# A list schedule for five engines: a price for every change of tile shape on TensorE, and a table that shifts streams of work in the order

## The chip, the cores and the metric

The kernel runs on one core of a Trainium2 chip. Time is in device microseconds (us) of one execution, lower is better. The engines are named as the profile names them: PE is TensorE (matmul), PEld its weight loads, DVE is VectorE, ACT is ScalarE, POOL is GpSimd, and SP issues the DMAs. Each engine works through its own row of instructions in order and waits on semaphores for the others.

## The reference

Two layers of a transformer block over 1024 tokens of width 1024, in float32. Each layer takes a normed and modulated copy of x, projects it, runs three mixers on it, and adds their result and that of a gated feed-forward to x:

```python
for l in range(DEPTH):
    mod = jax.nn.silu(c) @ ada_w[l] + ada_b[l]
    sh1, sc1, g1, sh2, sc2, g2 = jnp.split(mod[:, None, :], 6, axis=-1)
    h = rms_norm(x, norm1_g[l]) * (1.0 + sc1) + sh1
    z = h @ w_in[l]
    ...
    o_a = dsa_mixer(...)
    o_b = rwkv7_mixer(...)
    o_c = nsa_mixer(...)
    mixed = jnp.concatenate([o_a, o_b, o_c], axis=-1) @ w_out[l]
    x = x + g1 * mixed
    h = rms_norm(x, norm2_g[l]) * (1.0 + sc2) + sh2
    gate, up = jnp.split(h @ ffn_wi[l], 2, axis=-1)
    x = x + g2 * ((jax.nn.silu(gate) * up) @ ffn_wo[l])
```

dsa_mixer is an attention over the 256 best keys of each query by an index score. rwkv7_mixer is a linear recurrence with a 64 x 64 state for each of 8 heads. nsa_mixer adds up an attention over compressed blocks, one over the 16 best blocks and one over a window of 512.

## The kernel before

**Tiling and stages.** The tokens are worked in two halves of 512, with the width on the partitions: x is eight tiles of 128 x 512. A dense product (`dense`) adds up in one accumulator `mm` of 128 x 512, of which there are two. Each operand is split into a high and a low part in fp32r (`whi`, `wlo` from a loaded tile `wraw`; `hh`, `hl` from the normed x; `acthi`, `actlo` and `ohi`, `olo` likewise), and each product is three matmuls: high by high, low by high, high by low. The stages of the main stream are `("D", l, h)`, the projection of half h in layer l, and `("F", l, h)`, output projection and feed-forward, in the order D00, D01, F00, D10, F01, D11, F10, F11.

**The other streams.** The attention blocks (tiles `at`, `p`, `pt`, `pT`, `po`), the units of the recurrence (`am`, `X`, `TX`, `av`, `WU`, `MN`, `S`, `Y`), the top-k searches (`score`, `junk`, `sel`, `tk_...`), and the modulation of the second layer (`macc`, sums of loaded tiles `ada` on DVE) run as streams of their own beside the main one. A norm (`norm`) is a stream too: PE sums the squares `nsq` into `ss`, DVE takes the inverse root in twelve short steps on `ss` and `nex`, PE broadcasts it as `rb`, and DVE and ACT make `nt`, `hh` and `hl` of it. The small steps on PE use a part of the array: S, X, TX are 64 x 64, `po` and Y 128 x 64, `ss` 128 x 32. In the scan S, each of eight steps needs `sh`, which DVE makes of the step before. `z` is made in two halves: ACT writes one (`z<-mm,omu`), DVE adds the other (`z<-mm,vec,z`) and by that frees the accumulator.

**What sets the order.** The kernel runs its streams twice through generators. The first run plans buffers; in the second, `Program` records every instruction with its dependencies in the order in which the streams were taken up (`Rec`, numbered `r.n`). `Program.order` then makes the final order: a list schedule that steps through the five engines, and on each takes, of the records whose operands are ready, the one with the lowest number. `Chip` holds its prices. On PE, `Chip.is_part` tells a record on the full array from one on a part of it; if the next record is of the other kind, one of the present kind that stands at most LATER = 100 numbers behind is taken first. A change from full to part is charged 0.095 us and one back 0.045, the first full record after a part is charged 0.105 more, and a change between two part shapes nothing. `Program.issue` (line 697) writes all instructions out, so every row of the trace has that line and is told by its tiles.

Of the kernel before, what the change touches and what calls it, by code (L numbers as in the profile page):

```python
# [497 lines left out]
class Rec:  # L498
    __slots__ = ("key", "name", "a", "k", "cost", "deps", "n", "users", "pe", "func", "port", "prio")

# [20 lines left out]
class Program:  # L521
# [32 lines left out]
    def add(self, key, name, a, k, aps, outs, cost, pe=None, port=False):  # L554
        r = Rec()
        r.key, r.name, r.a, r.k, r.cost, r.pe, r.port = key, name, a, k, cost, pe, port
        r.n, r.deps, r.users = len(self.recs), set(), []
        r.prio = self.weave.cur.prio
        r.func = a[2] if key == "S" and name == "activation" else None
# [45 lines left out]
    def order(self):  # L605

        recs, chip, LATER = self.recs, Chip(), 100

        kinds, begun = ([], []), set()
        missing = [len(r.deps) for r in recs]
        for r in recs:
            for d in r.deps:
                recs[d].users.append(r.n)
        ready = {e: [] for e in ENGINES}
        coming = {e: [] for e in ENGINES}
        at = [0.0] * len(recs)
        for r in recs:
            if not missing[r.n]:  # L620
                heapq.heappush(coming[r.key], (0.0, r.n))
        out = []
        while len(out) < len(recs):
            best = None
            for e in ENGINES:
                t = chip.free[e]
                if not ready[e]:
                    if not coming[e]:
                        continue
                    t = max(t, coming[e][0][0])  # L630
                while coming[e] and coming[e][0][0] <= t:
                    n = heapq.heappop(coming[e])[1]
                    heapq.heappush(ready[e], n)
                    if e == "PE":
                        heapq.heappush(kinds[Chip.is_part(recs[n])], n)
# [7 lines left out]
                s = max(chip.start(recs[n]), at[n])  # L643
                if s > t + 0.1 and recs[n].port:

                    for m in heapq.nsmallest(8, ready[e])[1:]:
                        if not recs[m].port and t + recs[m].cost < s + 0.1:
                            n, s = m, max(t, at[m])
                            break
                if best is None or s < best[0]:  # L650
                    best = (s, e, n)
            s, e, n = best
            if ready[e][0] == n:
                heapq.heappop(ready[e])
            else:
                ready[e].remove(n)
                heapq.heapify(ready[e])
            if e == "PE":
                begun.add(n)
            end = chip.put(recs[n], s)  # L660
            out.append((s, n))
            for u in recs[n].users:
                v = recs[u]
                at[u] = max(at[u], chip.after(recs[n], v, s, end))
                missing[u] -= 1
                if not missing[u]:
                    heapq.heappush(coming[v.key], (at[u], u))
# [30 lines left out]


ENGINES = ("PE", "V", "S", "G", "D")  # L700


class Chip:
# [5 lines left out]
    def __init__(self):  # L709
        self.free = {e: 0.0 for e in ENGINES}  # L710
        self.cells = [[0.0] * 4 for _ in range(4)]
        self.part, self.first = False, False
# [4 lines left out]
    def is_part(r):  # L717
        rows, cols, _ = r.pe
        return rows[1] - rows[0] + cols[1] - cols[0] < 8

    def start(self, r):

        t = self.free[r.key]
        if r.key == "PE":
            rows, cols, _ = r.pe
            part = self.is_part(r)
# [7 lines left out]
    def put(self, r, s):  # L734

        if r.key == "PE":
            rows, cols, c = r.pe
            while s >= (self.stretch + 1) * self.STRETCH:
# [3 lines left out]
                self.stretch += 1  # L742
            part = self.is_part(r)
# [5 lines left out]
            self.first = part  # L749
            share = 1.0 if not part else (rows[1] - rows[0]) * (cols[1] - cols[0]) / 16.0  # L750
# [7 lines left out]
            self.part = part  # L758
            self.free["PE"] = s + step + more
# [1765 lines left out]
```

## Time and profile before

| | us |
|---|---|
| median of 3 runs | 3439.8 |
| lowest and highest run | 3438.86, 3444.59 |
| profiled execution, its own time | 3442.7 |
| span of the profiled execution | 3441.0 |

The profile has the busy time of each engine, a timeline of instructions with the idle time before each and what ended it, and tables of stretches. A start on PE comes before the end of the matmul ahead, since matmuls are pipelined; the time from start to start is what a matmul takes of PE. PEclk is the granted clock as a share of 2.4 GHz; its two levels are 1.2 and 2.4 GHz. Matmuls in plain float32 stand in the trace as two records each, transposes and fp32r ones as one.

### The profile page before, as it was taken

To read this page: it belongs to the slowest core of one execution; us is meant where nothing else is said; L and a number is where in the kernel's file an instruction comes from. 1 tells how busy PE (TensorE), PEld (TensorE's weight loads), DVE (VectorE), ACT (ScalarE), POOL (GpSimd) and SP (SyncE) were. 2 spreads that over 40 slices of the span, in tenths; PEclk is the share of its full clock that TensorE was granted. 3 is DMA by queue.
4 is the path that set the end of the run, shared out by engine and by line. 5 is a ranking of instruction groups with operands and counts; after the bars stand their busy time and mean duration, and the time that the engine had idled before them with its cause. 6 is when DMAs were issued, how large, how long until landed. Compare 5 with 4: busy or idle time off the path is not lost. (4 is left out here: it accounts for less than half of the span.)

```text
span 3441.0 us, 58566 instructions
## 1 busy us (share of the span) xinstructions
PE 3215.3 (93%) x20564; PEld 2496.7 (73%) x20564; DVE 2176.2 (63%) x5705; ACT 1775.1 (52%) x3706; POOL 1488.3 (43%) x1235
## 2 busy tenths in 40 slices
PE   6898999989999998889899999899799999999999
PEld 3656776767767776767678887677577787778887
DVE  4688988898899634698952114698888853241112
ACT  3445566756674643545464234567777454343232
POOL 2433453434335444442434554443343344445554
PEclk8999999989999998999899999899999999999999
DMA  8684345445523243554223333463232222423333
GB/s 280 197 260 124 108 138 160 145 138 161 194 77 108 70 131 113 154 157 118 74 67 115 98 97 114 145 189 122 67 86 67 84 80 80 144 91 96 98 95 98
DMA packets 354755, 424.99 MB, mean 124 GB/s; under 512 B 129686, under 2 KB 167190, under 8 KB 354460
## 3 DMA queue, kind: packets, MB, share of 16 engines
q1 hardware_dynamic: 354460, 421.25, 39.9%
q8 instruction: 162, 2.65, 0.3%
q14 instruction: 133, 1.09, 0.1%
HBM read 347.06 MB, written 60.44 MB: 118 GB/s over the span
## 5 line engine op out<-in xcount | busy, mean ns | idle before, releaser
L697 POOL TENSOR_TENSOR wlo<-wraw,whi 128x512 fp32r<-128x512 f32 (+1 forms) x808 | 1072.1, 1329 | 1346.1 <-ACT whi L697 1243.1
L697 ACT ACTIVATE whi<-wraw 128x512 fp32r<-128x512 f32 (+1 forms) x808 | 500.7, 622 | 993.9 <-PE mm L697 664.6
L697 PE MATMUL mm<-hh,whi 128*128 128x512 f32 x2144 | 865.9, 405 | 38.5 <-ACT hh L697 10.4
L697 PE MATMUL mm<-hh,wlo 128*128 128x512 f32 x2128 | 847.9, 399 | 5.5 <-POOL wlo L697 5.4
L697 PE MATMUL mm<-hl,whi 128*128 128x512 f32 x2112 | 843.7, 400 | 5.5 <-DVE hl L697 3.2
L697 PEld LDWEIGHTS mm<-hh,whi 128*128 128x128 f32 x2144 | 410.5, 192 | 141.2 <-issue 16.1
L697 PEld LDWEIGHTS mm<-hh,wlo 128*128 128x128 f32 x2128 | 407.1, 191 | 101.0 <-POOL wlo L697 10.1
L697 PEld LDWEIGHTS mm<-hl,whi 128*128 128x128 f32 x2112 | 404.3, 191 | 94.6 <-issue 8.2
L697 DVE TENSOR_TENSOR sg<-sg,mm 128x512 f32<-128x512 f32 x87 | 59.5, 684 | 474.0 <-PE mm L697 473.8
L697 DVE SCALAR_TENSOR_TENSOR x<-mm,mod,x 128x512 f32<-128x512 f32 x232 | 172.9, 747 | 245.5 <-PE mm L697 244.5
L697 PE MATMUL mm<-acthi,whi 128*128 128x512 f32 x704 | 280.4, 402 | 13.9 <-DVE x L697 5.8
L697 PE MATMUL mm<-actlo,whi 128*128 128x512 f32 x704 | 277.6, 397 | 1.9 <-POOL actlo L697 1.8
L697 PE MATMUL mm<-acthi,wlo 128*128 128x512 f32 x704 | 276.6, 396 | 0.0
L697 ACT ACTIVATE p<-p,nb,rst 128x512 f32<-128x512 f32 (+3 forms) x256 | 170.6, 667 | 62.0 <-DVE nb L697 60.7
L697 ACT ACTIVATE junka<-score,tk_nt 128x512 int8<-128x512 f32 x240 | 165.9, 691 | 21.5 <-DVE tk_nt L697 16.0
L697 PEld LDWEIGHTS mm<-acthi,whi 128*128 128x128 f32 x704 | 133.3, 190 | 49.8 <-DVE x L697 6.8
L697 ACT COPY pT<-pt 128x512 f32<-128x512 f32 (+2 forms) x220 | 121.8, 588 | 70.3 <-PE pt L697 50.4
L697 PEld LDWEIGHTS mm<-actlo,whi 128*128 128x128 f32 x704 | 133.4, 190 | 31.2 <-POOL actlo L697 6.7
L697 PEld LDWEIGHTS mm<-acthi,wlo 128*128 128x128 f32 x704 | 133.5, 190 | 27.4 <-issue 0.2
L697 DVE TENSOR_SCALAR p<-p,rs 128x512 f32<-128x512 f32 (+3 forms) x288 | 151.9, 579 | 1.5 <-issue 0.9
L697 PE MATMUL pt<-c_ident,p 128*128 128x128 f32 x816 | 134.9, 282 | 14.3 <-DVE p L697 6.7
L697 PEld LDWEIGHTS pt<-c_ident,p 128*128 128x128 f32 x816 | 100.9, 143 | 48.8 <-issue 11.8
(386 smaller groups left out, 5916.7 us busy)
## 6 DMA issues: line engine op xcount, KB each, us to landing
wraw<-in_wi_dram SPq DMA_DIRECT2D x352, 256.0 KB, 2.6
ada<-in_ada_dram SPq DMA_DIRECT2D x192, 256.0 KB, 4.4
wraw<-in_win_dram SPq DMA_DIRECT2D x184, 256.0 KB, 3.2
wraw<-in_wo_dram SPq DMA_DIRECT2D x160, 256.0 KB, 2.6
x<-x SPq DMA_DIRECT2D x64, 256.0 KB, 3.7
w<-in_w_dram SPq DMA_DIRECT2D x64, 256.0 KB, 3.8
wraw<-in_wout_dram SPq DMA_DIRECT2D x64, 256.0 KB, 2.8
o_in<-o SPq DMA_DIRECT2D x32, 256.0 KB, 3.5
```

Of the source, the lines that this page charges most:

```text
L697: getattr(engines[r.key], r.name)(*[real(x) for x in r.a], **{n: real(x) for n, x in r.k.items()})
```

## The change

Nothing that is computed changes, and no tile, buffer or dependency; only the order that `Program.order` makes. Two parts of it change.

First, `Chip` tells shapes apart by rows and columns (`shape_of`) and not only full from part. Any change of shape is charged 0.095 us at its start, a full record after a change 0.105 more and a part record after a change 0.05, and a record of the present shape that stands at most 100 places behind is taken ahead of one of another shape.

Second, a record's place in line is no longer its number. Each record knows the scope of its stream (`r.scope`), and a table SHIFTS with some 110 entries adds an amount to the number of every record of a scope; the records are ranked anew by that (`rank`, `pos`). A scope ("F", 0, 0), "child", 2 is the second stream that the stage F00 started.

```diff
@@ Program.order
+        size, seen, place = {}, {}, []
+        for r in recs:
+            size[r.scope] = size.get(r.scope, 0) + 1
+        for r in recs:
+            k = seen[r.scope] = seen.get(r.scope, -1) + 1
+            by = SHIFTS.get(r.scope, (0,))
+            place.append((r.n + by[k * len(by) // size[r.scope]], r.n))
+        rank = [n for _, n in sorted(place)]
...
-                n = ready[e][0]
-                if e == "PE" and Chip.is_part(recs[n]) != chip.part:
-                    same = kinds[chip.part]
+                q = ready[e][0]
+                if e == "PE" and Chip.shape_of(recs[rank[q]]) != chip.shape:
+                    same = kinds.get(chip.shape)
                     while same and same[0] in begun:
                         heapq.heappop(same)
-                    if same and same[0] - n <= LATER:
-                        n = same[0]
+                    if same and same[0] - q <= LATER:
+                        q = same[0]
...
+SHIFTS = {
+    (('F', 0, 0), 'child', 2): (-298,), (('F', 0, 1), 'child', 1): (-20,), (('F', 0, 1), 'child', 2): (-55,),
...
+    (('F', 1, 1), 'child', 2): (-652,), ('F', 0, 0): (-99,), ('F', 0, 1): (2,), ('F', 1, 0): (6,),
...
@@ Chip
-        return rows[1] - rows[0] + cols[1] - cols[0] < 8
+        return rows[1] - rows[0], cols[1] - cols[0]
...
-            return t + (0.0 if part == self.part else 0.095 if part else 0.045)
+            return t + (0.0 if self.shape_of(r) == self.shape else 0.095)
...
-            more = 0.105 if not part and self.first else 0.0
...
-            step = c if not part or r.a[1].dtype != F32 else c / 2 + (0.0 if self.first else 0.05)
+            shape = self.shape_of(r)
+            part, changed = shape != (4, 4), shape != self.shape
+            more = 0.105 if changed and not part else 0.0
...
+            step = c if not part or r.a[1].dtype != F32 else c / 2
+            if part and changed:
+                step += 0.05
```

Three places show what becomes of the order. Numbers at the end of names tell instances apart; they differ between the two programs. The first is PE in the recurrence unit at 907 us, where S is the scan, po an attention's output and mm a dense product. Before:

```order
L697 MATMUL S_10811<-S_4718,MT_10656 64x64 x2
L697 MATMUL po_9928<-pT_10747,tm_127 64x256 x2
L697 MATMUL po_9928<-pT_10754,tm_4121 64x256
L697 MATMUL S_10811<-sh_10817,MT_10656 64x64 x2
L697 MATMUL po_9928<-pT_10754,tm_4121 64x256
L697 MATMUL po_9928<-pT_10776,tm_4121 64x256 x2
L697 MATMUL S_10811<-sh_10817,MT_10656 64x64 x2
L697 MATMUL po_9928<-pT_10826,tm_4089 64x256 x2
```

And after:

```order
L711 MATMUL S_10962<-S_4719,MT_10806 64x64 x2
L711 MATMUL po_9974<-pT_10917,tm_4092 64x256 x2
L711 MATMUL S_10962<-sh_10970,MT_10806 64x64 x2
L711 MATMUL mm_10945<-hh_9242,wlo_10802 128x512
L711 MATMUL mm_10945<-hh_9254,whi_10782 128x512
L711 MATMUL mm_10945<-hl_9260,whi_10782 128x512
L711 MATMUL mm_10945<-hh_9254,wlo_10802 128x512
L711 MATMUL mm_10945<-hh_9262,whi_10782 128x512
L711 MATMUL mm_10945<-hl_9275,whi_10782 128x512
L711 MATMUL S_10962<-sh_10970,MT_10806 64x64 x2
```

The po rows went elsewhere, and six dense rows stand between the second and the third S step where po rows of another shape stood. Over the whole order of PE, changes between a full and a part shape and back rise from 326 to 357 pairs, and changes between two part shapes fall from 266 to 164.

The second place is DVE at the norm of F00, around 765 us, where ss and nex are the chain of the norm and macc the modulation of the second layer. Before:

```order
L697 SCALAR_TENSOR_TENSOR macc_9152<-ada_9232,silu_c,macc_9152 128x512
L697 TENSOR_SCALAR m_2115_9255<-m_2115_9255 128x1
L697 SCALAR_TENSOR_TENSOR macc_9152<-ada_9118,silu_c,macc_9152 128x512
L697 TENSOR_SCALAR nb_9274<-m_2115_9255,rst_1832 128x1
L697 SCALAR_TENSOR_TENSOR macc_9152<-ada_9157,silu_c,macc_9152 128x512
L697 SCALAR_TENSOR_TENSOR nex_9204<-ss_9174,nex_9204 128x128
L697 SCALAR_TENSOR_TENSOR macc_9152<-ada_9264,silu_c,macc_9152 128x512
L697 SCALAR_TENSOR_TENSOR ss_9174<-ss_9174,nex_9204 128x128
L697 TENSOR_SCALAR macc_9284<-ada_9186,silu_c 128x512
L697 TENSOR_TENSOR ss_9174<-ss_9174,nex_9204 128x128
L697 TENSOR_TENSOR A_9289<-am_9242,c_msi 128x512
L697 SCALAR_TENSOR_TENSOR nex_9204<-ss_9174,nex_9204 128x128
```

And after:

```order
L711 TENSOR_TENSOR ss_9128<-ss_9128,nex_9149 128x128
L711 TENSOR_SCALAR junk_5859,tk_cn_1500_5860<-sel_6655,tk_tr_1507_85 128x128
L711 SCALAR_TENSOR_TENSOR nex_9149<-ss_9128,nex_9149 128x128
L711 SCALAR_TENSOR_TENSOR f_9053<-r_8955,vec,k_2076_9170 128x512
L711 ISA p_9186,m_2085_9106<-at_9174,c_mask 128x256
L711 ISA m_2085_9106 128x1
L711 SCALAR_TENSOR_TENSOR ss_9128<-ss_9128,nex_9149 128x128
L711 TENSOR_SCALAR m_2085_9106<-m_2085_9106 128x1
L711 TENSOR_TENSOR ss_9128<-ss_9128,nex_9149 128x128
L711 TENSOR_SCALAR nb_9197<-m_2085_9106,rst_1901 128x1
L711 SCALAR_TENSOR_TENSOR nex_9149<-ss_9128,nex_9149 128x128
```

Both pieces end with the chain's last step. The macc rows between the steps are gone; from the chain's first row to its last there are 40 rows before and 34 after.

The third is DVE at 2272 us, in front of the step that frees the accumulator mm (the row with `z<-mm`), with rows of the top-k ahead of it. Before:

```order
L697 TENSOR_SCALAR score_24234<-score_24234,tk_sg_5535_24682 128x512
L697 TENSOR_SCALAR score_24369<-score_24369,tk_sg_5535_24682 128x384
L697 TENSOR_SCALAR junk_24043,tk_cn_5534_24044<-sel_24760,tk_tr_5541_89 128x512
L697 SCALAR_TENSOR_TENSOR ssk_24673<-ssk_24673,kex_24771 128x128
L697 TENSOR_SCALAR score_24425<-score_24425,tk_sg_5535_24682 128x512
L697 TENSOR_TENSOR ssk_24673<-ssk_24673,kex_24771 128x128
L697 SCALAR_TENSOR_TENSOR z_24714<-mm_24599,vec,z_24714 128x511
```

And after:

```order
L711 TENSOR_SCALAR score_24216<-score_24216,tk_sg_5535_24611 128x512
L711 TENSOR_SCALAR score_24317<-score_24317,tk_sg_5535_24611 128x384
L711 TENSOR_SCALAR score_24385<-score_24385,tk_sg_5535_24611 128x512
L711 TENSOR_SCALAR score_24478<-score_24478,tk_sg_5535_24611 128x512
L711 TENSOR_TENSOR q_24630<-rt_24670,rot_24646 128x512
L711 TENSOR_SCALAR kex_24776<-ssk_24699 128x128
L711 SCALAR_TENSOR_TENSOR z_24726<-mm_24615,vec,z_24726 128x511
```

Here one more score row stands ahead of z than before.

## Rows read from the trace of the kernel before

**Rows 1.** The page, part 1: busy us of each engine, share of span, instructions

```profile
span 3441.0 us, 58566 instructions
...
PE 3215.3 (93%) x20564; PEld 2496.7 (73%) x20564; DVE 2176.2 (63%) x5705; ACT 1775.1 (52%) x3706; POOL 1488.3 (43%) x1235
```

**Rows 2.** Stretches (us; PE, PEld, DVE, ACT, POOL busy; PEclk, DMA share, GB/s), closing feed-forward

```profile
2889.00:3441.00 552.00, 531.72 (x2356) 433.01 (x2354) 131.73 (x184) 178.58 (x298) 264.31 (x211) 0.98 0.32 103
```

**Rows 3.** Stretches, the three parts in which rows move, and their sum

```profile
118.00:1263.00 1145.00, 1071.41 (x7867) 805.58 (x7866) 947.12 (x2652) 675.71 (x1505) 474.70 (x396) 0.96 0.47 144
...
1428.00:1894.00 466.00, 437.31 (x3380) 343.54 (x3379) 340.23 (x995) 232.03 (x495) 201.05 (x172) 0.97 0.38 110
...
2190.00:2889.00 699.00, 661.12 (x4574) 514.19 (x4574) 543.09 (x1527) 461.83 (x1015) 282.24 (x231) 0.97 0.34 103
...
sum 2310.00, PE 2169.84 PEld 1663.31 DVE 1830.44 ACT 1369.57 POOL 957.99; mean PE 723.28 PEld 554.44 DVE 610.15 ACT 456.52 POOL 319.33
```

**Rows 4.** Stretches, around three norms and around the longest wait

```profile
337.00:363.00 26.00, 17.47 (x164) 14.80 (x162) 26.00 (x70) 9.13 (x21) 12.68 (x13) 0.74 0.21 69
...
740.00:782.00 42.00, 26.38 (x106) 18.91 (x105) 40.54 (x95) 14.22 (x29) 16.55 (x14) 0.59 0.40 125
...
2263.00:2275.00 12.00, 4.56 (x18) 3.05 (x17) 10.50 (x30) 5.12 (x10) 6.36 (x5) 0.79 0.62 202
...
2440.00:2476.00 36.00, 21.31 (x133) 15.08 (x134) 33.04 (x101) 24.95 (x54) 8.24 (x7) 0.76 0.27 75
```

**Rows 5.** Timeline of PE (start, us, op, shapes, xcount, idle before), scan of S

```profile
907.02 0.33 PE L697 MATMUL S<-S,MT 64*64 64x64 f32 x4
...
907.29 1.08 PE L697 MATMUL po<-pT,tm 128*64 128x256 f32 x6
...
917.64 0.39 PE L697 MATMUL mm<-hl,whi 128*128 128x512 f32 x1
...
917.87 0.39 PE L697 MATMUL mm<-hh,wlo 128*128 128x512 f32 x1
...
918.19 0.33 PE L697 MATMUL S<-sh,MT 64*64 64x64 f32 x4
...
918.45 0.50 PE L697 MATMUL mm<-hh,whi 128*128 128x512 f32 x1
...
918.78 0.39 PE L697 MATMUL mm<-hl,whi 128*128 128x512 f32 x1
...
922.42 0.48 PE L697 MATMUL S<-sh,MT 64*64 64x64 f32 x4 [3.00 <-DVE sh L697]
```

**Rows 6.** Timeline of PE, a run of one part shape

```profile
335.11 1.15 PE L697 MATMUL TX<-X,Tt 64*64 64x64 f32 x32 [0.22 <-ACT X L697]
...
336.19 0.45 PE L697 MATMUL at<-K,Qhi 128*128 128x384 f32 x1
```

**Rows 7.** Groups of ACT: count, busy us, mean ns, idle before

```profile
L697 ACT ACT_TABLE_LOAD x61 | 78.3, 1283 | 6.3 <-DVE nb L697 4.6 <-PEq L2515 0.7
```

**Rows 8.** Timeline of PE, norm of the first feed-forward

```profile
751.37 0.65 PE L697 MATMUL ss<-nsq,c_ident 128*32 128x128 f32 x8
...
770.13 2.07 PE L697 MATMUL rb<-nex,c_sel 128*128 128x128 f32 x8
```

**Rows 9.** Timeline of DVE, same stretch, one of eight such rows

```profile
761.36 0.74 DVE L697 SCALAR_TENSOR_TENSOR macc<-ada,silu_c,macc 128x512 f32<-128x512 f32 x1
```

**Rows 10.** Waits of PE (us in total, times, longest us), 118:1263, then whole span

```profile
PE mm L697 <- DVE x L697: 3.2, 2, 3.0
...
PE mod L697 <- DMA ada<-in_ada_dram: 4.5, 3, 3.3
...
PE mm L697 <- DVE z L697: 10.5, 6, 6.4
```

**Rows 11.** Timelines of ACT and of PE around the longest wait

```profile
2263.09 0.63 ACT L697 ACTIVATE whi<-wraw 128x512 fp32r<-128x512 f32 x1 [5.91 <-DMA wraw<-in_win_dram]
...
2273.48 0.80 PE L697 MATMUL mm<-hh,whi 128*128 128x512 f32 x1 [6.43 <-DVE z L697]
```

More of the change, by code (lines that the diff above doesn't have):

```diff
@@ L498 @@
 class Rec:
-    __slots__ = ("key", "name", "a", "k", "cost", "deps", "n", "users", "pe", "func", "port", "prio")
+    __slots__ = ("key", "name", "a", "k", "cost", "deps", "n", "users", "pe", "func", "port", "prio", "scope")
 def spread(offset, dims, unit):
@@ L609, in order @@
         recs, chip, LATER = self.recs, Chip(), 100
-        kinds, begun = ([], []), set()
+        size, seen, place = {}, {}, []
[6 more added lines that the diff above has]
+        rank = [n for _, n in sorted(place)]
+        pos = [0] * len(recs)
+        for k, n in enumerate(rank):
+            pos[n] = k
+        kinds, begun = {}, set()
         missing = [len(r.deps) for r in recs]
@@ L620, in order @@
             if not missing[r.n]:
-                heapq.heappush(coming[r.key], (0.0, r.n))
+                heapq.heappush(coming[r.key], (0.0, pos[r.n]))
         out = []
@@ L631, in order @@
                 while coming[e] and coming[e][0][0] <= t:
[L632 to L633 removed]
+                    q = heapq.heappop(coming[e])[1]
+                    heapq.heappush(ready[e], q)
                     if e == "PE":
[L635 to L638 removed]
+                        heapq.heappush(kinds.setdefault(Chip.shape_of(recs[rank[q]]), []), q)
+                q = ready[e][0]
+                if e == "PE" and Chip.shape_of(recs[rank[q]]) != chip.shape:
+                    same = kinds.get(chip.shape)
                     while same and same[0] in begun:
                         heapq.heappop(same)
[L641 to L644 removed]
+                    if same and same[0] - q <= LATER:
+                        q = same[0]
+                r = recs[rank[q]]
+                s = max(chip.start(r), at[r.n])
+                if s > t + 0.1 and r.port:
                     for m in heapq.nsmallest(8, ready[e])[1:]:
[L647 to L648 removed]
+                        r = recs[rank[m]]
+                        if not r.port and t + r.cost < s + 0.1:
+                            q, s = m, max(t, at[r.n])
                             break
                 if best is None or s < best[0]:
[L651 to L653 removed]
+                    best = (s, e, q)
+            s, e, q = best
+            if ready[e][0] == q:
                 heapq.heappop(ready[e])
             else:
[L656 removed]
+                ready[e].remove(q)
                 heapq.heapify(ready[e])
             if e == "PE":
[L659 removed]
+                begun.add(q)
+            n = rank[q]
             end = chip.put(recs[n], s)
@@ L711, in __init__ @@
         self.cells = [[0.0] * 4 for _ in range(4)]
-        self.part, self.first = False, False
+        self.shape = 4, 4
         self.port, self.wire, self.table, self.ring = 0.0, 0.0, None, [0.0] * 8
@@ L742, in put @@
                 self.stretch += 1
-            part = self.is_part(r)
-            more = 0.105 if not part and self.first else 0.0
-            step = c if not part or r.a[1].dtype != F32 else c / 2 + (0.0 if self.first else 0.05)
+            shape = self.shape_of(r)
+            part, changed = shape != (4, 4), shape != self.shape
+            more = 0.105 if changed and not part else 0.0
+            step = c if not part or r.a[1].dtype != F32 else c / 2
+            if part and changed:
+                step += 0.05
             if part and cols[1] - cols[0] == 1:
                 step = 0.014
-            self.first = part
             share = 1.0 if not part else (rows[1] - rows[0]) * (cols[1] - cols[0]) / 16.0
@@ L757, in put @@
                     self.cells[i][cols[0]:cols[1]] = [s + c + more] * (cols[1] - cols[0])
-            self.part = part
+            self.shape = shape
             self.free["PE"] = s + step + more
```

15 lines of the change are left out of this document (11 added, 4 removed), and 27 rows, old and new, of the table SHIFTS.

## Prediction

> **What bounds the kernel now.** I read the busy shares first. TensorE (PE) is busy for 3215.3 of 3441.0 us, VectorE (DVE) for 2176.2 [rows 1]. That leaves PE 225.7 us without work, but the share is an average over stages with different limits, so the next view is the one by stretches. The change moves work in the order only; every instruction of before is still there, plus four table loads on ScalarE. Comparing the two orders on PE, four stretches hardly change: 0 to 118, 1263 to 1428, 1894 to 2190 and 2889 to 3441 us, 1131 us together, with 3215.3 - 2169.8 = 1045.5 us of PE work [rows 1, 3]. In the last of them, the closing feed-forward, PE is the bound: 531.7 of 552 us busy, DVE 131.7 [rows 2]. I expect nothing from these 1131 us in either direction.
>
> The other 2310 us are where rows move. There PE is busy for 2169.8 us and idle for 140.2, and DVE is busy for 1830.4, that is 79% [rows 3]. The granted clock is 0.96, 0.97 and 0.97 in the three parts [rows 3]. At the lower of the two levels (1.2 instead of 2.4 GHz) PE spent about 2 x 0.04 x 1145 + 2 x 0.03 x 466 + 2 x 0.03 x 699 = 162 us. Short stages hold much of both: around the three norms inside the moved part (337 to 363, 740 to 782, 2440 to 2476) PE is busy 65.2 of 104 us at clocks 0.74, 0.59 and 0.76 while DVE is busy for 99.6 [rows 4]. There DVE is the bound, and its order decides when PE gets work. So at most 140 us of idle time and half of 162 us of clock are on offer, and the DVE's load keeps most of it out of reach.
>
> **Part one: the new prices and keeping to one shape.** Before, the planner told only full-array matmuls (128 x 128) from the rest. The S steps (64x64) and po steps (128x64) could alternate at no price to it. The trace prices this. Dense steps start 0.23 us apart (917.64 to 917.87); from a dense step to S it is 0.32, from the pair of S matmuls to the next dense step 0.26, and from that to the second one 0.33 [rows 5]. Sixteen TX matmuls of the same shape take 1.08 us with a change at their end [rows 6], so a pair without one takes at most 0.13. A trip from full to part and back therefore costs about 0.09 + 0.14 + 0.10 = 0.33 us. From S to po it is 0.27 [rows 5], so a change between two part shapes costs about 0.15. Counted over the whole orders, trips rise from 326 to 357 and changes between part shapes fall from 266 to 164. The sum is 31 x 0.33 - 102 x 0.15 = 10.2 - 15.3 = -5 us. If every part-to-part change was hidden under another wait, +10 remains; if the extra trips fall into waits, -15. I take -5, since in rows 5 the steps on either side follow with no wait. The four table loads, 1.28 us each by the mean of the 61 there are [rows 7], are 5 us on ScalarE, which is busy for 52% of the span [rows 1]; I take them as hidden behind its idle time, and at +5 if not.
>
> **Part two: the shifted streams.** Three things can be read at named places.
>
> The norms. Before the first feed-forward, PE sums the squares at 751.37 and can broadcast the result only at 770.13 [rows 8]: 18.8 us for a chain of twelve short DVE steps (ss, nex). The order before puts eight macc rows in between, 0.74 us each for the full ones [rows 9], which belong to the other layer. After the change none is there; 34 rows stand in the chain and not 40. Adding the rows' own mean durations in the trace, the chain falls from 18.5 to about 11 us. Counted alike, the chain at 2442 falls from 17 to 9 us and the one at 358 from 8 to 5. That is 19 us off three chains. DVE's work is not less by it, it is put behind the chain, next to dense work of PE. PE was idle for 38.8 us in these stages [rows 4], not all of it for the chain, so I take half: -10, with bounds 0 and -19.
>
> Single waits. Of the 101 us of idle time in the moved part outside these stages, the long waits are few: S for sh 3.00 at 922.42 [rows 5], mm for x 3.0, mod for its load 3.3 [rows 10], and mm for z 6.43 [rows 11]. In the new order the S step that waited has 18 dense rows between it and its forerunner instead of three, and another group of dense matmuls stands before the mm that waited for x. For z nothing is better (below), and mod waits for a load. So 6.0 of 15.7 us goes, 38%. Of 101 us that is -38. But a row that is pulled forward pushes others back, and waits that the trace does not show can open; the trace has no row for them. The bound above is that they give all of it back and more, +20, as three waits like that for z would. I take -15.
>
> The clock. 0.41 x 2 x 42 + 0.24 x 2 x 36 + 0.26 x 2 x 26 = 65 of the 162 us at the lower level lie in the three norm stages [rows 4], each after PE had stood idle for some us. With 0.5 us lost for each of them in which PE works (63% of the time), they cost 20 us; if the shorter chains keep 40% of that, -8. Bounds: 0, and -24 if 30% of all 162 us goes.
>
> **What does not get better.** At 2273.48 PE waits 6.43 us, the longest wait of the trace, for z, the DVE step that frees its accumulator [rows 11]. ScalarE had waited 5.91 us for a weight load, until 2263.09 [rows 11], and writes its part of that z only after; DVE then has rows of the top-k (score, junk) ahead of its own step. In the new order four score rows stand straight ahead of z, where there were three. I count this wait as staying.
>
> **The sum.** -5 - 10 - 15 - 8 = -38 us against the profiled execution, which took 3442.7 us (span 3441.0 and 1.7 around it): 3405. That execution is 2.9 us above the median of the runs, 3439.8, so the forecast on the median's footing is 3402; I say 3403.
>
> **Rivals.**
> *Nothing measurable.* The shape part is -5, and what the norms win on PE was DVE's time anyway: DVE is busy 40.5 of 42 us at 740 [rows 4], so the dense work that starts earlier meets the macc rows that were put behind, and waits for its own DVE steps there. Then -5 alone is left, 3435, within 0.2% (the 6.9 us that a measurement of this kernel can tell from no change). For it: the great steps of the program stand at nearly the same place of the PE order as before. Against: macc is not on the path of the stage that follows. Chance 0.12.
> *Slower: a moved step blocks its queue.* ScalarE and DVE took their rows in order at 2263: whi waited 5.91 us for its load, and z, whose matmul had ended, stood behind it until PE stopped for 6.43 us [rows 11]. The new order moves rows on these engines in every moved stretch, by a plan that knows no late load. Each such place costs its 6.4 us and some 3 us at the lower clock after it (0.79 over 2263 to 2275 [rows 4]), about 10. Up to three new places eat the gains of norms, waits and shape (30 us); from four on it is slower, and at five it is 3440 - 30 + 50 = 3460. For it: the longest wait of the trace is of this kind. Against: of PE's six waits for z this one is 6.4 us and the other five are 4.1 together [rows 10], so most moved rows of this kind hold nobody up. Chance 0.13. The Trainium skill, page "TensorE: Matmul & The Clock Gate", in its section "Architectural detail: the array is 16× 32×32, not 1× 128×128", says that ScalarE and VectorE are strict FIFO, with no reordering; by that rule an early row with a late operand always holds up what is behind it, and the time of this rival would follow. The trace agrees as far as 2263 goes.
> *More than forecast.* 38% of all 140 us of idle time and 30% of the clock's 81 us go, and the shape part gives -5: -53 - 24 - 5 = -82, 3360. Chance 0.10.
>
> **How the numbers follow.** Forecast 3403 with 0.65 for its surroundings (3375 to 3432), 0.10 for more, 0.12 for nothing measurable, 0.13 for slower. Faster than 3433: 0.75; within 0.2%: 0.12; slower than 3447: 0.13. The low end is the larger gain, 3360; the high end takes in the same case and the beginning of the slower one, 3450, which leaves out about 0.1 on either side.
>
> **What would show it.** In the profile after: the span from the first ss to rb at the first feed-forward near 11 us instead of 18.8; PE busier than 26.4 of 42 us there and a clock above 0.59; the S wait and the mm wait for x gone; the wait for z still there; the four untouched stretches as long as before, with the difference all made by 1890 us and between 2190 and 2890. PE's busy time barely lower. Wrong would be: the norm stages shorter, but new waits of PE for DVE or ScalarE of several us in 800 to 1260 or 2500 to 2890; or untouched stretches that differ, which would mean that loads, not the order, set the time.

## The result, and the profile after

The changed kernel takes 3405.8 us (median of 4 runs, 3398.09 to 3409.64) against 3441.1 (4 runs); the ratio is 0.9894, with a 95% interval of 0.9878 to 0.991. The forecast was 3403. The total is right, but as the rest shows its terms are not. Spans, stretches and waits below are read from one execution of each kernel; the four of the changed kernel lie 11.6 us apart.

The page of the changed kernel, part 1, to be held against [rows 1]:

```profile
span 3406.6 us, 58570 instructions
...
PE 3187.4 (94%) x20564; PEld 2473.6 (73%) x20564; DVE 2148.7 (63%) x5705; ACT 1784.5 (52%) x3710; POOL 1490.1 (44%) x1235
```

PE's busy time fell by 27.9 us and its idle time only from 225.7 to 219.2, by 6.5. I had expected the reverse: of the 38 us forecast, 25 were idle time (norms and waits) and 13 busy time (shape and clock). The granted clock over the whole span went from 0.965 to 0.973; 2 x (1 - clock) x span is the time at the lower level, 241 us before and 184 after (from the rounded clock, good to 3 us).

Next, where it happened. The stretches here are cut at the start of the same PE steps in both programs, so a row of one answers to the row of the other, but for work that was moved across a cut. Columns as in [rows 2]. Before:

```profile
108.00:368.50 260.50, 234.73 (x1795) 164.28 (x1793) 209.96 (x697) 123.85 (x282) 94.55 (x88) 0.94 0.60 188
368.50:694.80 326.30, 314.52 (x2576) 237.76 (x2573) 281.36 (x783) 218.61 (x512) 143.22 (x119) 0.99 0.48 141
694.80:1337.70 642.90, 598.85 (x3859) 463.59 (x3857) 479.07 (x1203) 367.06 (x772) 273.99 (x221) 0.96 0.41 127
1337.70:1900.00 562.30, 520.61 (x3815) 409.58 (x3816) 387.93 (x1080) 278.25 (x579) 245.85 (x206) 0.95 0.38 112
1900.00:2912.30 1012.30, 960.48 (x5925) 758.24 (x5924) 637.69 (x1662) 575.00 (x1203) 438.88 (x353) 0.97 0.34 103
2912.30:3441.00 528.70, 508.42 (x2253) 413.72 (x2251) 127.87 (x179) 171.11 (x287) 253.15 (x202) 0.98 0.33 103
```

And after:

```profile
107.10:364.90 257.80, 225.98 (x1795) 158.75 (x1793) 208.03 (x699) 124.03 (x282) 94.95 (x88) 0.95 0.61 190
364.90:687.20 322.30, 304.11 (x2467) 231.53 (x2464) 271.60 (x768) 215.23 (x495) 143.15 (x119) 0.99 0.48 143
687.20:1314.20 627.00, 594.44 (x3964) 460.63 (x3963) 472.62 (x1217) 374.69 (x792) 270.23 (x222) 0.98 0.43 131
1314.20:1867.80 553.60, 515.35 (x3816) 404.18 (x3817) 388.11 (x1080) 281.51 (x580) 247.74 (x206) 0.95 0.39 114
1867.80:2881.60 1013.80, 964.87 (x5925) 758.52 (x5924) 628.52 (x1662) 576.72 (x1204) 442.18 (x353) 0.97 0.34 102
2881.60:3406.60 525.00, 505.56 (x2253) 410.80 (x2251) 128.14 (x179) 171.28 (x287) 253.71 (x202) 0.99 0.33 104
```

| stretch (times of before) | length | PE busy | PE idle (length less busy) |
|---|---|---|---|
| 108 to 368 | -2.7 | -8.8 | +6.1 |
| 368 to 695 | -4.0 | -10.4 | +6.4 |
| 695 to 1338 | **-15.9** | -4.4 | **-11.5** |
| 1338 to 1900 | -8.7 | -5.3 | -3.4 |
| 1900 to 2912 | +1.5 | +4.4 | -2.9 |
| 2912 to the end | -3.7 | -2.9 | -0.8 |

Almost half of the gain is made in one stretch, that of the norm before the first feed-forward. It is rather more: the second row of after has 109 PE records fewer (x2467 against x2576) and the third 105 more. These are steps of one recurrence unit (MN, PT) that now stand behind the cut, 0.03 to 0.04 us each in the traces, with a few others about 5 us. At equal work the second stretch is thus no shorter, and the third some 21 us. The second layer from 1900 us on, where I expected a part of it, gives 2 us. And ahead of the norm idle time rose by 12.5 us.

How far can such a row be trusted? Two kernels below (longer chain, DVE rows behind it) keep this order and add steps in the third stretch alone. Their other stretches take 254.4 and 256.9, 326.3 and 329.9, 551.4 and 546.0, 1012.0 and 1005.4, 524.6 and 524.3 us. One order thus varies by some 8 us in a stretch, and only the third row of the table is clear of that. The fourth is in doubt: kernels below that are no faster than before take 556.7, 549.6 and 543.8 us for it (prices only, table only, entries of layer 1), so it may be the 562.3 of before that stands out.

The norm of 751 us stood before as in [rows 8], that of 2442 us so (timeline of PE, columns as in [rows 5]):

```profile
2442.41 0.42 PE L697 MATMUL ss<-nsq,c_ident 128*32 128x128 f32 x8 [3.28 <-DVE nsq L697]
...
2462.03 1.05 PE L697 MATMUL rb<-nex,c_sel 128*128 128x128 f32 x8
```

And now:

```profile
743.32 0.66 PE L711 MATMUL ss<-nsq,c_ident 128*32 128x128 f32 x8 [1.78 <-DVE nsq L711]
...
752.23 1.63 PE L711 MATMUL rb<-nex,c_sel 128*128 128x128 f32 x8 [0.18 <-DVE nex L711]
...
2416.98 0.66 PE L711 MATMUL ss<-nsq,c_ident 128*32 128x128 f32 x8 [3.75 <-DVE nsq L711]
...
2423.64 2.01 PE L711 MATMUL rb<-nex,c_sel 128*128 128x128 f32 x8
```

From ss to rb it takes 8.9 us instead of 18.8, and 6.7 instead of 19.6. The clock around the first of them and around the scan S, as stretches of after:

```profile
732.00:774.00 42.00, 27.93 (x141) 19.21 (x140) 38.58 (x106) 22.47 (x43) 21.05 (x17) 0.76 0.49 157
...
905.00:930.00 25.00, 23.89 (x161) 17.69 (x160) 23.05 (x57) 16.53 (x32) 8.59 (x8) 1.00 0.83 270
```

Around the S wait of [rows 5] the kernel before had this stretch:

```profile
917.00:929.00 12.00, 9.00 (x64) 6.70 (x63) 10.30 (x22) 5.52 (x9) 4.32 (x3) 0.72 0.58 180
```

In 42 us the clock was 0.59 [rows 4] and is 0.76: 34 us at 1.2 GHz became 20. Around the scan S, where PE had stood idle for 3.00 us, another 7 us at the lower level are gone.

The waits of PE, as in [rows 10], over the whole span of after:

```profile
PE mm L711 <- DVE z L711: 3.8, 3, 1.6
```

Over 118 to 1263, those of S before:

```profile
PE S L697 <- DVE sh L697: 4.3, 3, 3.0
```

And over the same window after:

```profile
PE xt L711 <- DVE x L711: 6.9, 1, 6.9
PE S L711 <- DVE sh L711: 5.3, 7, 1.9
...
PE mm L711 <- DVE x L711: 3.2, 4, 1.2
...
PE mod L711 <- DMA ada<-in_ada_dram: 0.9, 2, 0.6
```

All four long waits that I had named are shorter (S 1.9 at most, x 1.2, z 1.6, mod in this window 0.6). But S now waits seven times where it waited three, 5.3 us in all and not 4.3, and a wait of 6.9 us is new: at 340.83 PE stands before a transpose of x (xt) until DVE, busy with short rows of other streams, comes to its copy of x.

### The profile page after: what moved, and what is told of

It reads as the page before. It is cut to its first block, busy times and chain, and to the rows that moved or that the text cites. A ratio compares the mean times of both kernels' runs of the same rounds, so it can differ in the third digit from the quotient of the medians.

```text
span 3406.6 us, 58570 instructions
## 1 busy us (share of the span) xinstructions
PE 3187.4 (94%) x20564; PEld 2473.6 (73%) x20564; DVE 2148.7 (63%) x5705; ACT 1784.5 (52%) x3710; POOL 1490.1 (44%) x1235
## 5 line engine op out<-in xcount | busy, mean ns | idle before, releaser
L711 PE MATMUL pt<-c_ident,p 128*128 128x128 f32 x816 | 140.8, 281 | 14.2 <-DVE p L711 11.7
```

The lines of the kernel that those rows point to most:

```text
L711: getattr(engines[r.key], r.name)(*[real(x) for x in r.a], **{n: real(x) for n, x in r.k.items()})
```

## The experiments

Each kernel is the changed one with one edit; edits of the table are written entry by entry. Ratios are against the kernel before, on the same chip, with their 95% interval; the median of before was 3441.1 us beside the change and 3436 to 3438 beside the others, so medians of different rows compare to some 5 us. "Trips" are changes full-part-full, "p-p" changes between two part shapes; time at 1.2 GHz is from the mean clock, as above.

| run | median us | ratio | interval | trips | p-p | at 1.2 GHz |
|---|---|---|---|---|---|---|
| the change | 3405.8 | 0.9894 | 0.9878-0.991 | 357 | 164 | 184 |
| prices only | 3444.1 | 1.0022 | 1.0008-1.0035 | 326 | 183 | 234 |
| table only | 3471.0 | 1.0095 | 1.0078-1.0112 | 354 | 278 | 222 |
| without four norm entries | 3404.7 | 0.9906 | 0.9889-0.9922 | 356 | 164 | 184 |
| entries of layer 0 | 3414.3 | 0.9925 | 0.9903-0.9947 | 338 | 168 | 190 |
| entries of layer 1 | 3438.0 | 0.9999 | 0.9987-1.001 | 345 | 176 | 234 |
| amounts dealt at random | 3496.3 | 1.0165 | 1.0143-1.0188 | 389 | 163 | 287 |
| amounts x 0.8 | 3414.0 | 0.9935 | 0.9922-0.9949 | 347 | 171 | 212 |
| without two entries | 3465.5 | 1.008 | 1.0063-1.0097 | 341 | 185 | 250 |
| LATER = -1 | 3801.4 | 1.1055 | 1.1035-1.1076 | 989 | 184 | 388 |
| LATER = 300 | 3462.9 | 1.0076 | 1.0058-1.0094 | 309 | 176 | 235 |
| chain longer | 3444.4 | 1.0023 | 1.0005-1.004 | 357 | 164 | 213 |
| DVE rows behind it | 3436.0 | 1.0 | 0.9984-1.0015 | 357 | 164 | 192 |

### The two halves apart

```diff
 SHIFTS = {
-    (('F', 0, 0), 'child', 2): (-298,), (('F', 0, 1), 'child', 1): (-20,), (('F', 0, 1), 'child', 2): (-55,),
...
 }
```

> The new prices and the keeping to one shape, with an empty table. Against the kernel before, the order of PE has as many trips full-part-full (326) and 83 fewer changes between part shapes (266 to 183). By the prediction's price of 0.15 us a change that is -12 us of PE's own time. Theory P (the gain of 35 us is made by the prices, with the clock following from steadier work): 3408 to 3420 us. Theory T (the table makes it, the prices only their own 12 us or less): 3428 to 3440. Of the lower clock, P expects the 50 us less time at 1.2 GHz that the changed kernel showed, T at most 15 us less.

For the table alone, `Chip` and the choice on PE are those of before:

```diff
-                if e == "PE" and Chip.shape_of(recs[rank[q]]) != chip.shape:
-                    same = kinds.get(chip.shape)
+                if e == "PE" and Chip.is_part(recs[rank[q]]) != chip.part:
+                    same = kinds.get(chip.part)
```

> The table of shifts, with the prices and the keeping of before (full and part only). Trips go from 326 to 354, changes between part shapes from 266 to 278: by the prediction's prices +9 and +2 us of PE's own time. Theory P (prices make the gain): 3435 to 3455, no faster than before. Theory T (the table makes it, by waits and clock): 3410 to 3425. If the two parts add up, the gains of this kernel and of the one with prices alone sum to 35 us; if the table is tuned to the order that the new prices give, they sum to clearly less.

Neither theory held. Prices alone are 0.2% slower than before, the table alone 1.0% slower, and together they are 1.1% faster. The parts don't add: the table fits the order that the new prices give, and not that of the old ones. Stretches of the kernel with prices alone, the second and third of the table above and 368 to 500 us:

```profile
369.60:707.30 337.70, 317.46 (x2572) 239.72 (x2569) 270.19 (x777) 219.86 (x514) 138.94 (x119) 0.97 0.46 136
707.30:1347.20 639.90, 591.41 (x3863) 462.12 (x3861) 482.51 (x1204) 372.43 (x775) 268.24 (x221) 0.97 0.41 128
...
368.00:500.00 132.00, 121.78 (x1041) 94.23 (x1035) 95.04 (x239) 77.07 (x168) 55.24 (x49) 0.92 0.40 111
```

And 368 to 500 us of the changed kernel:

```profile
368.00:500.00 132.00, 122.70 (x1023) 94.39 (x1022) 108.74 (x261) 82.26 (x176) 69.26 (x55) 0.99 0.43 125
```

With prices alone PE keeps to its shape, and over the whole span its busy time falls from 3215.3 to 3198.9 us; but its idle time rises from 225.7 to 244.1 and takes it all back. The 368 to 695 stretch takes 337.7 us instead of 322.3 (5 of them work that the table moves behind the cut). In the 132 us from 368 on DVE gets 95 us of work where it gets 109 in the changed kernel and 113 in the one before, and PE runs at 0.92 and not 0.99 (before 0.97). So I read it that what the prices save in shape changes (83 x 0.15 = 12 us) they pay with DVE's work coming late, and that the table undoes that; no run separates it.

### What a change of shape costs

```diff
-        recs, chip, LATER = self.recs, Chip(), 100
+        recs, chip, LATER = self.recs, Chip(), -1
```

> The changed kernel with LATER = -1 in place of 100: PE never keeps to its shape, it takes the lowest place at once. Trips full-part-full go from 357 to 989, changes between part shapes from 164 to 184. This prices a trip on the path: at 0.33 us each, 632 trips and 20 changes are 209 + 3 = 212 us, 3618 us. If half of the trips fall into waits of PE or only take the place of them, 3510; if trips are dearer together with the clock (the prediction's prices are of full clock), 3650 and more.

3801 us: 395 us for 632 more trips and 20 more p-p, 0.62 us each. The single steps have the prices of the prediction. In its timeline of PE, with WU 64x64:

```profile
999.57 0.43 PE L711 MATMUL WU<-rhs,Tt 64*64 64x128 f32 x2
999.93 0.49 PE L711 MATMUL mm<-acthi,wlo 128*128 128x512 f32 x1
1000.36 0.65 PE L711 MATMUL WU<-rhs,Tt 64*64 64x128 f32 x8
1000.94 0.50 PE L711 MATMUL mm<-acthi,whi 128*128 128x512 f32 x1
1001.28 0.40 PE L711 MATMUL mm<-actlo,whi 128*128 128x512 f32 x1
1001.52 0.40 PE L711 MATMUL mm<-acthi,wlo 128*128 128x512 f32 x1
```

A dense step between two part steps takes 0.43 us from start to start (999.93 to 1000.36), the first one after a part 0.34, others 0.23 to 0.24. Medians over three traces (before, the change, this kernel) at full clock: full to part +0.09 and +0.05 on the first part step, part to full +0.10 and +0.11 on the first full one, 0.35 in all; part to part 0.10 + 0.05 = 0.15. What makes 0.62 of 0.35? There are 204 us more at the lower clock, which cost about half of that, 102 us, and idle time rose by 43. That leaves some 250 us, 0.40 for each trip. In part it is above 0.35 because many trips here are for a single small step, which is dearer: one S between dense steps takes 0.255 us (median of 42 places in this trace), two in a row 0.262; one am (64x128) takes 0.415, and 0.11 in a row of them.

```diff
-        recs, chip, LATER = self.recs, Chip(), 100
+        recs, chip, LATER = self.recs, Chip(), 300
```

> The changed kernel with LATER = 300: PE keeps to its shape over 300 places and not 100. Trips go from 357 to 309, changes between part shapes from 164 to 176. The run with LATER = -1 had 632 more trips and was 395 us longer, 0.62 us each. If the price holds here, 48 trips less and 12 changes more are -28 us: 3378. If only PE's own time counts (0.33 each), -14: 3392. If the work that is put off up to 300 places makes others wait, and the table is tuned to 100: 3410 to 3440.

48 trips less, and 57 us slower, more than the last line of the expectation gave it (3440). As that line has it, the work that is put off makes others wait: PE is idle for 267.8 us and not 219.2. A part of it may be that the table was made for 100, which no run here separates.

### Which entries

```diff
-    (('F', 0, 0), 'child', 2): (-298,),
-    (('F', 0, 1), 'child', 2): (-55,),
-    (('F', 1, 0), 'child', 2): (-347,),
-    (('F', 1, 1), 'child', 2): (-652,),
```

> The changed kernel without the table's four entries that pull the norm streams of F00, F01, F10 and F11 forward (-298, -55, -347, -652). Theory G (the norm chains got shorter by 10 and 13 us, but DVE gives it back in the dense work behind, as the starts of later steps in the two traces suggest): 3402 to 3412, no difference to 3406. The prediction's step (half of the shortening reaches the end, 10 us over three chains): 3413 to 3418. All of it on the path: 3425 to 3432.

No difference, but the run does not test what I wrote. These are other streams than I took them for: child 2 of F00 and of F01 is the norm of the next projection, at 1338 and 2138 us of before, and its chain takes 4.7 and 4.8 us with the entry and without. The norm at 751 us is child 1 of F00 and has no entry; its chain is 8.9 us here too. So it became shorter by what was done to others.

For the next two, only the entries stay whose scope belongs to the first layer, or to the second. Of the first of them:

```diff
-    (('F', 1, 0), 'child', 1): (-226,),
-    (('F', 1, 1), 'child', 1): (14,),
...
-    (('D', 1, 0), 'child', 3): (2,),
...
```

> The changed kernel with only the 51 table entries of the first layer's streams. The run with prices alone came out at 1.002 of before, the one with the table alone at 1.010, and both together at 0.989: the gain belongs to neither part alone. In the trace of the changed kernel 32 of the 34 us are made before 1905 us, in the first layer. Theory L (these entries remove the waits that the new prices open there, each stretch for itself): 3403 to 3413. Rival W (the table is tuned as a whole, and entries of one layer alone move the rest off): 3425 to 3450.

> The changed kernel with only the 56 entries of the second layer. Theory L: as with prices alone up to about 1700 us (there +10 to +20 us against before at 640 to 900 us, 0 to +5 at 1700), and in the second layer about as good as the changed kernel, which gained 2 us there: 3434 to 3446. Rival W: 3450 to 3475, like the table without its prices.

Theory L holds: the first layer's entries alone give 0.9925, with an interval that just overlaps that of the whole change, those of the second alone nothing. With the first layer's entries the three stretches from 108 us on take 254.7, 322.2 and 627.5 us, as in the changed kernel; with prices alone they took 263.4, 337.7 and 639.9. The first of the two also says something on the norm at 2442 us. Its timeline of PE there:

```profile
2410.34 0.49 PE L711 MATMUL ss<-nsq,c_ident 128*32 128x128 f32 x8 [2.63 <-DVE nsq L711]
2424.38 0.83 PE L711 MATMUL rb<-nex,c_sel 128*128 128x128 f32 x6
```

And its stretch from 1900 us of before on:

```profile
1863.90:2873.80 1009.90, 957.28 (x5925) 755.51 (x5924) 630.93 (x1662) 574.48 (x1204) 444.15 (x353) 0.98 0.34 103
```

Without the second layer's entries the chain takes 14.0 us instead of 6.7, and the stretch 1009.9 instead of 1013.8. A gain of the shorter chain does not show there; one smaller than the 8 us or so by which a stretch varies could hide. Nor does the length of this chain tell the stretch elsewhere: kernels with 6.7, 7.6, 14.0, 19.6, 21.0 and 23.7 us (the change, layer 1, layer 0, before, prices only, without two entries) take 1014, 1017, 1010, 1012, 1011 and 1021 us for it.

```diff
-    (('F', 0, 0), 'child', 2): (-298,),
+    (('F', 0, 0), 'child', 2): (-41,),
...
-    'first': (-798,),
+    'first': (28,),
...
```

> The changed kernel with the same 107 scopes and the same 107 amounts, dealt out to the scopes at random. Trips full-part-full 389, changes between part shapes 163. Theory C (the table's amounts were chosen for these streams; with other amounts waits open): slower than prices alone (3444), 3455 to 3520; 32 more trips than in the changed kernel at the 0.62 us that a trip cost in the run without keeping are 20 us of it. Rival R (any loosening of the numbers' order gives the scheduler room and wins with the new prices): 3400 to 3430.

Theory C: 1.65% slower than before. Movement as such wins nothing, as far as one dealing shows.

```diff
-    (('F', 0, 0), 'child', 2): (-298,),
+    (('F', 0, 0), 'child', 2): (-238,),
...
```

> The changed kernel with every amount of the table at 0.8 of its value. Directions and streams are the same, the places differ a little. Theory M (each entry has a mechanism: it takes a stream out of the way of another): most of the gain stays, 3403 to 3418. Theory F (the table is fitted to one order to the last place, and loses its gain off that place, like the amounts dealt at random, 1.017 of before, and LATER = 300, 1.008): 3425 to 3470.

0.9935: theory M, six tenths of the gain stay. Directions count, and the last fifth of the amounts is worth 0.4%.

### The norm and DVE

```diff
-    ('first', 'child', 9): (151,),
-    (('F', 1, 0), 'child', 1): (-226,),
```

> The changed kernel without two entries: that of the modulation stream whose macc rows stood in the norm chain before the first feed-forward (+151), and that of the norm stream at 2442 us (-226). The run without the four 'child 2' entries touched other norms, in stretches where PE is the bound; these two are the ones that move the chains that got shorter by 10 and 13 us. Trips 341, changes between part shapes 185, 16 trips fewer and 21 such changes more than in the changed kernel, about equal in price. Theory G (given back): 3402 to 3412. The prediction's step (half reaches the end): 3414 to 3420. If the macc rows also hold PE and the clock up behind the norm, as in the kernel before (clock 0.96 over 750 to 1263, 0.99 after the change): 3420 to 3435.

Two of 107 entries gone, and the kernel is 60 us slower, more than any of my lines. Its norm before the first feed-forward, in the timeline of PE:

```profile
782.71 0.66 PE L711 MATMUL ss<-nsq,c_ident 128*32 128x128 f32 x8 [1.21 <-DVE nsq L711]
...
810.30 2.07 PE L711 MATMUL rb<-nex,c_sel 128*128 128x128 f32 x8
```

And its stretches from 368 and from 695 us of before on:

```profile
374.70:723.60 348.90, 318.40 (x2431) 240.78 (x2428) 276.21 (x781) 219.38 (x505) 139.78 (x118) 0.94 0.45 131
723.60:1373.70 650.10, 602.07 (x4003) 467.73 (x4005) 470.95 (x1201) 372.18 (x782) 272.50 (x222) 0.97 0.41 126
```

27.6 us from ss to rb, 18.7 more than in the changed kernel, and the stretch with it is 23.1 us longer (650.1 against 627.0, some 2 us of it work moved across the cut): no sign that this is given back. But 26.6 us are lost in the 349 us ahead of the norm, at a clock of 0.94, and 8.9 ahead of these. The modulation stream also issues 160 loads from 100 us on, and has PE steps among the attention work; so this run moves more than a chain.

The kernels with the new prices and LATER = 100 can be set side by side here. With a chain of 8.9 us (the change, without four norm entries, layer 0) this stretch takes 627.0, 630.4 and 627.5 us; with 12.3 (x 0.8) 628.6; with 14.2 (prices only, layer 1) 639.9 and 642.0; with 20.0 (dealt at random) 670.2; with 27.6 (this run) 650.1. The long chains go with the long stretches, but not by a fixed price, and each of these kernels differs in more than the chain.

The last pair keeps the order of the changed kernel and issues one step several times more, with the same operands and the same result. First it is nex from ss in the norm at 751 us (`first`), then a macc from ada some 50 us behind (the third of its kind):

```diff
+                getattr(engines[r.key], r.name)(*args, **kw)
...
+                    if first:
...
+                        for _ in range(100):
+                            getattr(engines[r.key], r.name)(*args, **kw)
```

> The changed kernel with its order kept, and one step of the norm chain before the first feed-forward (nex from ss, 128x128 on DVE, 0.20 us from start to start) issued 100 more times in place: the chain from ss to rb, 8.9 us, becomes 29 us, and DVE has 20 us more work. To be read against the run with the same 20 us of DVE work behind the chain. Theory G (DVE is the bound of this stretch, the chain's length is given back): both runs are longer by the same amount within 4 us. Rival N (the chain stands on PE's path, as the prediction's norm step has it): this run is 18 to 28 us longer than the changed kernel (the clock after the idle time among it), the other by 8 or less.

```diff
+                getattr(engines[r.key], r.name)(*args, **kw)
...
+                    if macc and seen == 3:
...
+                        for _ in range(50):
+                            getattr(engines[r.key], r.name)(*args, **kw)
```

> The changed kernel with its order kept, and one DVE step of the modulation (macc from ada, 128x512, 0.40 us from start to start) issued 50 more times, some 50 us behind the norm: 20 us more DVE work outside the chain. Theory G: as long as the run with the longer chain, 12 to 20 us over the changed kernel's 3406. Rival N: 0 to 8 us over it, since PE has dense work with its operands ready there.

The longer chain in the timelines of DVE and PE:

```profile
747.72 32.47 DVE L723 TENSOR_SCALAR nex<-ss 128x128 int32<-128x128 int32 x100
...
781.40 1.11 PE L713 MATMUL tk<-c_ident,y 128*128 128x128 f32 x4 [35.89 <-DVE y L713]
```

And the stretch from 695 us of before on:

```profile
688.90:1353.00 664.10, 595.94 (x3967) 462.01 (x3969) 500.42 (x1317) 374.91 (x792) 269.76 (x222) 0.96 0.40 123
```

The same timelines of the kernel with the later rows:

```profile
807.95 26.07 DVE L723 TENSOR_SCALAR macc<-ada,silu_c 128x512 f32<-128x512 f32 x50
...
834.69 0.80 PE L713 MATMUL bc<-fhi,blocks 128*128 128x512 f32 x1 [29.24 <-ACT pT L713]
```

And its stretch:

```profile
692.70:1350.10 657.40, 595.75 (x3967) 461.79 (x3965) 497.81 (x1267) 375.12 (x792) 270.24 (x222) 0.96 0.40 125
```

The additions were 32.5 and 26.1 us and not 20 (see the end). They cost the stretch 37.1 and 30.4 us (627.0 in the changed kernel), 1.14 and 1.17 times themselves, inside the chain and 50 us behind it; by the medians the kernels are some 39 and 30 us slower than the changed one. Theory G's equal cost holds for each us that was added. So one piece of 26 or 32 us of DVE time has no cover here in either place; PE has no spare dense work of that length at its turn, and the first step that waits is not the norm's but one of the top-k (tk) or the attention (bc). Rival N's 0 to 8 us for the later rows is refuted. What the pair can't tell is whether rows of 0.7 us, spread out, would have found cover: one piece of 26 us blocks PE wherever it stands.

## Why the prediction came out

**Sum.** -38 was forecast, -34.4 us of span measured. It is right by two errors against each other, that is by luck: idle time fell by 6.5 us where 25 were forecast, and busy time by 27.9 where 13 were. The two traces, counted by the level of the granted clock, take this apart. At 1.2 GHz PE was busy for 180.1 us before and 136.2 after, and idle for 59.0 and 49.4; at 2.4 GHz it was busy for 3035.2 and 3051.2, and idle for 166.6 and 169.9. A dense step takes 0.427 us at the lower level and 0.227 at the higher (medians in both traces). By that, as an estimate, some 21 us of the gain are steps that no longer run at the lower level and 10 are idle time that lay there; PE's own work is some 7 us less, and waits at full clock are 3 more.

**Shape, -5.** Near enough: the unit prices hold (0.33 was 0.35, 0.15 was 0.15), and 31 x 0.35 - 102 x 0.15 is -4.5, against some -7 by the estimate above. What I did not see is what the prices do without the table: what they save is lost again to waits, and the kernel comes out slower. The table loads, 65 now, are named in no wait of PE.

**Norms, -10.** The chains are about as short as forecast (8.9 for 11, 6.7 for 9, and 7.4 for 5 at 358 us). "Half of it reaches the end" is the mean of two places that behave differently. Around 751 us more than the 9.9 us of the chain came off: the stretch is 15.9 shorter, 11.5 of it idle time, and with a chain 18.7 us longer it is 23 us longer. That the chain alone does it is not shown: the table without the prices has a chain of 10.7 us there, and this stretch:

```profile
717.40:1369.50 652.10, 603.39 (x3963) 465.52 (x3961) 484.31 (x1229) 377.26 (x794) 277.36 (x222) 0.97 0.41 126
```

At 2442 us nothing came off that shows: +1.5 us over the stretch, and a chain twice as long made it no slower. In the rows of before the two differ by the clock, 0.59 at 740 and 0.76 at 2440 [rows 4]; whether that is why, no run tests.

**Waits, -15.** This step failed. It took the share of the named waits that would go, 38%, for the share of all idle time outside the norm stages. The two waits went, but outside the norm's stretch idle time is higher by 5.0 us (-6.5 in all, less the -11.5 there). A wait that a reader can name is not a sample of the others: new ones of the same kind opened, as xt for x and S for sh. And a named wait that goes need not be a gain: with prices alone S waits at most 1.4 us and mm for x 2.2, and that kernel is no faster. The bound of +20 held.

**z stays.** Wrong. It is 1.6 us now, and 1.3 to 2.8 in the traces of four kernels with the same or nearly the same order; ScalarE waits 2.75 us for its weight load there and not 5.91 [rows 11], in the timelines of ACT and PE of the changed kernel:

```profile
2233.02 0.63 ACT L711 ACTIVATE whi<-wraw 128x512 fp32r<-128x512 f32 x1 [2.75 <-DMA wraw<-in_win_dram]
...
2238.43 0.50 PE L711 MATMUL mm<-hh,whi 128*128 128x512 f32 x1 [1.56 <-DVE z L711]
```

I had read the order of the DVE rows, but by these rows the load was what came late. It made no difference that shows: the second layer gained 2 us.

**Clock, -8.** The direction was right, the size not: 241 to 184 us at the lower level, some 21 us for the steps alone. The stages behind the norm and the S wait (0.72 over 917 to 929) count as well, and I had counted only the norm stages.

**Untouched stretches.** 1905 to 2090 us of before takes the same time to 0.1 us. The closing feed-forward is 3 to 4 us shorter at the same order, at a clock of 0.99 and not 0.98. I had it at nothing, and nothing it may be: without four norm entries it takes 530.3 us, in the last pair 524.6 and 524.3.

**Rivals.** "Nothing measurable", with the norm's gain given back, fits what happened at 2442 and not at 751. "A moved step blocks its queue" happened once in the changed kernel, in the 6.9 us wait at 340.83, and three such places were needed to eat the gain. The experiments show that it was near: with other amounts in the same table it costs 1.65%, and my 0.13 for slower was for a risk that only the tuning of the table keeps away. That could not be read from the rows of before.

**Open.** Why the table with the old prices loses 1.0%: its chains are short (10.7 and 8.2 us), and yet each of the stretches from 108 to 1338 is longer than before, by 7, 15 and 9 us. Short norm chains alone are thus no gain. Its trace shows two long waits, tk for y at 349 us (8.6 us) and mm for z at 2291 (9.5 us), but no run tests them. Nor did I find which step of the modulation stream costs 27 us ahead of the norm when its entry is gone. DVE's busy time fell by 27.5 us with the same steps; no run explains that.

## What to carry to other kernels

A price in a list scheduler and a table of offsets that fits the order it gives are one change: measure them together, since here each alone lost and both together won. Judge a chain that got shorter by the length of the stretch it stands in, not by its own: one of the two here went with a gain larger than itself, clock included, the other with none that shows. Before reading a stretch, see by how much it differs between two traces of one order, here some 8 us. And do not scale up from the waits that one can name; a reordering moves waits, and here the idle time of the rest rose.

## What the hardware showed unexpectedly

A DVE step takes longer from start to start when the row behind it continues the same chain than when a row of another stream stands there. In the timeline of DVE of the changed kernel, first the norm at 1314 us, then that at 743:

```profile
1315.59 0.29 DVE L711 TENSOR_SCALAR nex<-ss 128x128 int32<-128x128 int32 x1
1315.91 0.30 DVE L711 SCALAR_TENSOR_TENSOR ss<-ss,nex 128x128 f32<-128x128 f32 x1
...
745.65 0.28 DVE L711 TENSOR_SCALAR nex<-ss 128x128 int32<-128x128 int32 x1
745.85 0.15 DVE L711 TENSOR_TENSOR ru<-ru,ry 128x8 f32<-128x8 f32 x1
```

The same step takes 0.32 us and 0.20. So the repeated steps of the last pair were dearer than I had counted: nex 0.32 (32.47 for 100), and macc (128x512) 0.52 (26.07 for 50) against 0.40 among other rows, 0.12 us more in both sizes.

On PE, the price of changes between shapes adds up for a dense step: a single one between two part steps takes 0.43 us and not 0.23 (0.09 and 0.11 more). For small steps the first is the dear one: a single S step between dense ones takes 0.255 us, two 0.262, and each further step of its shape 0.06.
